# Raw buffers filled ahead of the turned rows' writes, and attention's casts placed behind a norm's squares

## The chip, the cores and the metric

The kernel runs on one core of a Trainium2 chip. The metric is the device time of one execution in microseconds; three runs give a median. A profiled execution gives the trace from which the rows below are taken. In it PE is the matrix engine TensorE, DVE is VectorE, ACT is ScalarE, POOL is GpSimd, and SP is the engine whose queue issues nearly all transfers (its rows are marked SPq). An engine works through its own list of instructions in order, and each instruction waits for what it needs from the others.

## The reference

The program is a two-layer encoder trunk on 256 rows of 1024 float32 numbers. Layer 0 mixes tokens with a convolution module, layer 1 with multi-head latent attention. Each layer is

```
h += 1/2 * SwiGLU(RMSNorm(h))
h += Mixer(RMSNorm(h))
h += 1/2 * SwiGLU(RMSNorm(h))
```

and a last RMSNorm follows. The parts that matter here are the feed-forward and the entry of attention:

```
def swiglu_ffn(h, w1, w3, w2):
    return (jax.nn.silu(h @ w1) * (h @ w3)) @ w2          # 1024 -> 2816 -> 1024

a = h @ w_a                                               # 1024 -> 512 + 256 + 64
c_q  = rmsnorm(a[..., :512], g_q)
c_kv = rmsnorm(a[..., 512:768], g_kv)
k_rope = a[..., 768:]
q  = einsum("bsc,chd->bshd", c_q, w_uq)                   # 8 heads, 128 + 64 rotary
kv = einsum("bsc,chd->bshd", c_kv, w_ukv)                 # 8 heads, 128 keys + 128 values
```

## The kernel before, in words

**Rows and halves.** The 256 rows stand as two tiles `h[0]` and `h[1]` of 128 rows (`tb` 0 and 1). Products are made to full float32 accuracy from three products of rounded parts: a number is split into a high part `hi` and the rest `lo`, and `mm3` (L255) adds hi times lo, hi times hi and lo times hi.

**Weights.** All weights are read once, as a list of blocks of up to 128 x 2048 numbers (1 MB) in the order of use (`blocks`). `load` takes one block: a transfer into one of three raw buffers (`raw`, RAW_BUFS), and then two casts per block half, `hi` on ACT (L173) and `lo` = raw - hi on VectorE (L174), into one of five pairs of weight buffers (W_BUFS). A transfer waits until the raw buffer is free, which is when the `lo` cast of the block three before it has been done; a cast waits until the pair is free, which is when TensorE has finished with the block five before it. `weights(n)` hands out the next n blocks and `load_ahead` loads up to three more.

**Norms.** The RMS factor of a row is not applied to the rows ahead of the product; only the gain is, and the factor comes in behind it. `squares` sums the squares on ACT (L284, two halves), `power` adds the two sums and takes the power -1/2 on POOL (L292, L293, L295), each on one column of 128 numbers. In attention `normed` does the same for the query part (512 columns) and the key part (256) of the first product `a`, with one more POOL step (L1114), and then scales into `cn` on VectorE (L1116).

**Turning rows.** A product needs the rows transposed. For `h[0]` and the attention's parts `split_rows` does it on TensorE (`tp`, L301) and splits into `Xh` (ACT, L315) and `Xl` (VectorE, L319). In layer 1, for `h[1]` at the entries of the first feed-forward, of attention and of the last feed-forward, it goes by transfers: `turn_blocks` makes 32 x 32 transposes on VectorE (`ht`, L330), writes them in four transfers to a DRAM scratch (`hd`, L334) and reads them back in the turned order (`hb`, L336); `Norm.end` then splits `hb` into `Xh` (L397) and `Xl` (L398). This is done in two halves of 512 columns.

**The order around an entry.** `Rows.finish` ends a layer half: four accumulations (tb, d) one after the other, each followed by an addition into `h` (L566, L568) and then by `nxt.early(i)` of the next norm. `Norm.early` turns the first rows by TensorE and begins the turning by transfers (`begin`), the first half at i = 2 and the second at i = 3. Then the next half's first product starts. A feed-forward's `first_chunk` takes the row tiles in the order (w1, tb 0, all eight k), (w3, tb 0, four), (w1, tb 1, eight), (w3, tb 0, four), (w3, tb 1, eight), so that the turned rows are needed after 36 products of `mm3`. Attention takes query tb 0, key tb 0, query tb 1, key tb 1, and then the query's rotary part `qr`, between whose two row tiles stand the transposes of the second query norm and of both key norms (`CQ`, `CKh`, `CKl`). `X.late()` stands where the turned rows are split.

**What sets the order.** The code names the instructions in an order, and a scheduler with its own cost model settles each engine's final list. `urgent` marks functions whose instructions it shall take first; `behind` keeps casts behind the latest urgent work; `order(a, b)` puts a behind b, without any wait of its own where the two are on one engine. Weight transfers that are not needed yet are ordered behind the last `hb` read (`turns`).

Of the kernel before, what the change touches and what calls it, by code (L numbers as in the profile page):

```python
# [19 lines left out]
P = 128  # L20
# [6 lines left out]
HB = 2048  # L27
# [55 lines left out]
def trunk(ctx: ExitStack, tc: tile.TileContext, x, xt, pos, invf, gains, gfin, wdw,  # L83
# [14 lines left out]
    def uid(s):  # L98
        n_uid[0] += 1
        return f"{s}_{n_uid[0]}"  # L100
# [46 lines left out]
    turns = []  # L147
    last_read = [None]

    def load(src, pieces=1):  # L150
        if isinstance(src, tuple):
            raw = rawp.tile([P, HB], F32, tag="raw", name=uid("raw"))
            nc.sync.dma_start(raw, src[1])
            return raw
        n = src.shape[-1]
        raw = rawp.tile([P, HB], F32, tag="raw", name=uid("raw"))
        hi = wp.tile([P, HB], F32R, tag="hi", name=uid("hi"))
        lo = wp.tile([P, HB], F32R, tag="lo", name=uid("lo"))
        if len(loaded) < 7:

            for i in range(pieces if len(loaded) < 4 else 1):
                c = slice(i * n // pieces, (i + 1) * n // pieces) if len(loaded) < 4 else slice(n)
                fetch(raw[:, c], src[:, c])
        else:
            dma = nc.sync.dma_start(raw[:, :n], src)
            if turns and len(loaded) >= n_used[0]:

                order(dma, turns[-1].ins)
        for i in range(pieces):
            c = slice(i * n // pieces, (i + 1) * n // pieces)  # L170

            low = nc.gpsimd if len(loaded) == conv_block[-4] else nc.vector
            casts[len(loaded), i] = (nc.scalar.copy(hi[:, c], raw[:, c]),  # L173
                                     low.tensor_sub(lo[:, c], raw[:, c], hi[:, c].bitcast(F32)))  # L174
            for cast in casts[len(loaded), i]:
                behind(cast)
        return hi, lo
# [128 lines left out]
        return b  # L306

    @urgent
    def split_rows(src, q, n, gcol, dh, dl, tb, after=(), low_after=(), turned=None):

        b = transposed(src, q, n, after, turned)
        for j in range(n):
            k = q + j
            g = G[:, gcol + k:gcol + k + 1]
            high = nc.scalar.activation(dh[:, k, tbs(tb)], b[:, j * P:(j + 1) * P], AF.Copy, scale=g)  # L315
        for j in range(n):
            k = q + j
            g = G[:, gcol + k:gcol + k + 1]
            low = nc.vector.scalar_tensor_tensor(dl[:, k, tbs(tb)], b[:, j * P:(j + 1) * P], g,  # L319
                                                 dh[:, k, tbs(tb)].bitcast(F32), op0=ALU.mult, op1=ALU.subtract)  # L320
            for a in low_after:
                order(low, a.ins)
        return high

    def turn_blocks(pool, src, n, tag):


        w = n * P
        t = pool.tile([P, 512], F32, tag=tag + "t", name=uid(tag + "t"), bufs=2)
        nc.vector.transpose(t[:, :w], src.rearrange("p (t j q) -> p j t q", t=n, q=32))  # L330
        d = dram.tile([P, w], F32, tag=tag + "d", name=uid(tag + "d"), bufs=4)
        dv = d.rearrange("(j p) (i c) -> i p j c", p=32, c=32 * n)
        for i in range(4):
            nc.sync.dma_start(dv[i], t[32 * i:32 * i + 32, :w].rearrange("p (j c) -> p j c", j=4))  # L334
        b = pool.tile([P, 512], F32, tag=tag + "b", name=uid(tag + "b"), bufs=2)
        last_read[0] = nc.sync.dma_start(b[:, :w], d)  # L336
        return b[:, :w].rearrange("p (i t q) -> p t i q", i=4, q=32)

    class Norm:


        def __init__(self, gname, half=False, turn_by_dma=None):
            self.col = GCOL[gname]
            self.half = half

            self.pool = turn_by_dma
            self.turning = []
            self.whole = False
# [4 lines left out]
            self.turned = ()  # L353

            self.between = None

        def part(self, tb, q, after=(), low_after=()):
            turned = self.between if tb == 1 else self.turned if q == 0 and self.turned == [] else None
            self.high = split_rows(h[tb], 4 * q, 4, self.col, self.xh, self.xl, tb, after, low_after, turned)

        @urgent
        def rms(self, tb):
# [176 lines left out]
    class Rows:  # L539
# [20 lines left out]
        def finish(self, rh, make_next, act):  # L560
# [2 lines left out]

            def add(tb, c, o):
                if rh is None:
                    nc.vector.tensor_add(h[tb][:, c], o, h[tb][:, c])  # L566
# [36 lines left out]
    def ffn_in(act, X, make_next, beside):  # L603
# [11 lines left out]
        def first_chunk(X, u):  # L615

            kn = HB // 512
            parts = [weights(2, False) for m in range(2)]
            for m in range(2):
                for tb in range(NT):  # L620
                    u[m, tb] = bank("A", "u")
# [1 line left out]
            for n, (m, tb, ks) in enumerate(((0, 0, range(8)), (1, 0, range(4)), (0, 1, range(8)), (1, 0, range(4, 8)),  # L623
# [3 lines left out]
                elif n == 3:  # L627
                    load_ahead()
                for k in ks:
                    hi, lo = parts[m][k // kn]  # L630
# [448 lines left out]
    def mla_in(act, X, make_next, cc, sn):  # L1079
# [44 lines left out]
                rope(act, kd[:, i, :], kx.rearrange("p (n i f) -> p n i f", n=1, i=2), 1, cc, sn, tb)  # L1124
            return kd.rearrange("p i f -> p (i f)")

        parts = [weights(2, False) for _ in range(2)]
        cq, ck, kd = [], [], []
        last = None
        for tb in range(NT):  # L1130
            for i, w in enumerate((QL, KVL + ROPE)):
                u = low(parts[i], w, tb, last)
# [266 lines left out]
```

## Time and profile before

| | us |
|---|---|
| median of 3 runs | 932.98 |
| lowest and highest run | 931.16, 933.20 |
| the profiled execution, its own time | 932.56 |
| its span, first to last instruction | 930.8 |

The mean granted TensorE clock of the profiled execution is 0.991 of full speed. Times in the rows of a trace are microseconds from the start of the span. A row of the timeline has the start, the length, the engine, the line of the code, the operation, its output and inputs by name, their shape and a count, and in square brackets how long the engine stood idle ahead of it and who ended that. Rows of one kind that follow each other are merged into one, with their count. A row of the waits has the total, the number and the longest. "Granted clock" 0.50 means that TensorE ran at half speed.

### The profile page before, as it was taken

What the parts mean: (1) busy time and instruction counts of PE and PEld (TensorE: products, weight loads), DVE (VectorE), ACT (ScalarE), POOL (GpSimd) and SP (SyncE); (2) the same over time, 40 slices, a digit from 0 to 9 for tenths busy, and PEclk for the clock granted to TensorE, in tenths of its full rate; (3) what the DMA queues carried; (4) which work ended last, traced back from release to release, by engine and by line L of the source; (5) the groups of instructions that cost most, each with busy time, mean ns of one, the idle gap of its engine ahead of it and who ended that gap; (6) DMA issues with size and microseconds to landing.
All of it is one profiled execution on the core that took longest, in us unless ns stands there. A gap on an engine that the chain in (4) does not pass through costs nothing.

```text
span 930.8 us, 12107 instructions
## 1 busy us (share of the span) xinstructions
PE 917.0 (99%) x4346; PEld 768.8 (83%) x4346; DVE 590.2 (63%) x931; ACT 495.5 (53%) x844; POOL 125.5 (13%) x255
## 2 busy tenths in 40 slices
PE   9999999999999999999999999999799999999997
PEld 7888888898978888888888888888698888888886
DVE  5895754489987666654576566545846677656633
ACT  7664443488876444444454554444746575445421
POOL 1720000089941000000010000001300010000000
PEclk9999999999999999999999999999899999999999
DMA  9886775534227677775187776641841288776711
GB/s 342 309 313 223 296 239 207 181 137 165 68 87 271 232 250 247 244 238 208 64 309 288 238 265 240 226 174 39 322 137 46 91 308 308 242 234 233 257 45 46
DMA packets 65292, 194.73 MB, mean 209 GB/s; under 512 B 11856, under 2 KB 37072, under 8 KB 45904
## 3 DMA queue, kind: packets, MB, share of 16 engines
q1 hardware_dynamic: 64656, 193.27, 59.3%
q8 instruction: 34, 0.56, 0.2%
q10 hardware_dynamic: 576, 0.69, 0.2%
q14 instruction: 26, 0.21, 0.1%
HBM read 179.78 MB, written 14.16 MB: 208 GB/s over the span
## 4 chain that ended last, share of the span: by engine, by line
PE 93%; ACT 2%; DMA 1%; DVE 1%; POOL 1%; issue 1%; SPq 0%; POOLq 0%; ACTq 0%; DVEq 0%
PE u L261 17%; PE u L260 17%; PE u L257 17%; PE o L261 9%; PE o L260 9%; PE o L257 9%; PE u L718 3%; PE gate L718 3%; PE o L959 1%; PE u L266 1%; PE tp L301 1%; PE pairs L761 1%; PE nope L257 1%; PE nope L261 1%; PE nope L260 1%; PE sc L1208 1%
## 5 line engine op out<-in xcount | busy, mean ns | idle before, releaser
L174 DVE TENSOR_TENSOR lo<-raw,hi 128x1024 fp32r<-128x1024 f32 (+1 forms) x292 | 344.7, 1219 | 178.0 <-ACT hi L173 177.6
L173 ACT CAST hi<-raw 128x1024 fp32r<-128x1024 f32 x294 | 293.3, 1048 | 250.4 <-PE o L261 82.5
L261 PE MATMUL u<-hi,Xl 128*128 128x512 f32 x688 | 267.8, 389 | 0.3 <-DVE Xl L319 0.3
L257 PE MATMUL u<-lo,Xh 128*128 128x512 f32 x688 | 267.9, 389 | 0.0
L260 PE MATMUL u<-hi,Xh 128*128 128x512 f32 x688 | 267.7, 389 | 0.0
L261 PEld LDWEIGHTS u<-hi,Xl 128*128 128x128 f32 x688 | 129.1, 188 | 27.6 <-DVE Xl L319 0.7
L257 PEld LDWEIGHTS u<-lo,Xh 128*128 128x128 f32 x688 | 129.1, 188 | 26.9
L260 PEld LDWEIGHTS u<-hi,Xh 128*128 128x128 f32 x688 | 129.1, 188 | 26.7
L260 PE MATMUL o<-hi,Gh 128*128 128x512 f32 (+1 forms) x356 | 137.9, 387 | 0.0
L261 PE MATMUL o<-hi,Gl 128*128 128x512 f32 (+1 forms) x356 | 137.8, 387 | 0.0
L257 PE MATMUL o<-lo,Gh 128*128 128x512 f32 (+1 forms) x356 | 137.2, 387 | 0.0
L292 POOL TENSOR_TENSOR ms<-ss 128x1 f32<-128x1 f32 x16 | 10.9, 680 | 602.9 <-ACT junk L284 602.9
L257 PEld LDWEIGHTS o<-lo,Gh 128*128 128x128 f32 x356 | 66.9, 188 | 13.6
L260 PEld LDWEIGHTS o<-hi,Gh 128*128 128x128 f32 x356 | 66.9, 188 | 13.5
L261 PEld LDWEIGHTS o<-hi,Gl 128*128 128x128 f32 x356 | 66.9, 188 | 13.4
L613 DVE TENSOR_TENSOR Gl<-gb,Gh 128x512 fp32r<-128x512 f32 (+1 forms) x48 | 31.3, 652 | 57.3 <-ACT Gh L612 57.3
L612 ACT CAST Gh<-gb 128x512 fp32r<-128x512 f32 (+1 forms) x48 | 28.1, 585 | 73.7 <-DMA gb<-gd 73.7
L795 DVE SCALAR_TENSOR_TENSOR acc<-V,dw,acc 128x128 f32<-128x128 f32 (+1 forms) x176 | 54.6, 396 | 0.0
L816 ACT ACTIVATE prod<-V,dw 128x128 f32<-128x128 f32 (+1 forms) x129 | 46.2, 417 | 1.9 <-POOL Y L817 1.0
L686 DVE TENSOR_TENSOR s<-s,u 128x512 f32<-128x512 f32 (+1 forms) x48 | 30.6, 637 | 7.4 <-PE u L261 7.3
L685 ACT ACTIVATE s<-u,R 128x512 f32<-128x512 f32 (+1 forms) x48 | 31.2, 650 | 5.5 <-PE u L261 4.5
L817 POOL TENSOR_TENSOR odd<-odd,prod 128x128 f32<-128x128 f32 (+1 forms) x62 | 33.0, 536 | 0.0
(213 smaller groups left out, 871.8 us busy)
## 6 DMA issues: line engine op xcount, KB each, us to landing
raw<-in_f2w SPq DMA_DIRECT2D x66, 1024.0 KB, 5.0
raw<-in_f1w SPq DMA_DIRECT2D x62, 1024.0 KB, 5.3
raw<-in_cw SPq DMA_DIRECT2D x12, 1024.0 KB, 4.8
gd<-gt SPq DMA_DIRECT2D x160, 64.0 KB, 3.3
gb<-gd SPq DMA_DIRECT2D x40, 256.0 KB, 4.4
raw<-in_wo SPq DMA_DIRECT2D x4, 1024.0 KB, 4.8
raw<-in_wuq SPq DMA_DIRECT2D x3, 1024.0 KB, 4.8
raw<-in_f1w SPq DMA_DIRECT2D x8, 256.0 KB, 5.5
```

Source lines behind the costliest of these rows:

```text
L173: casts[len(loaded), i] = (nc.scalar.copy(hi[:, c], raw[:, c]), low.tensor_sub(lo[:, c], raw[:, c], hi[:, c].bitcast(F32)))
L174: low.tensor_sub(lo[:, c], raw[:, c], hi[:, c].bitcast(F32)))
L257: mm = nc.tensor.matmul(o, ah, bl, start=start, stop=False)
L260: nc.tensor.matmul(o, ah, bh, start=False, stop=False)
L261: return nc.tensor.matmul(o, al, bh, start=False, stop=stop)
L613: nc.vector.tensor_sub(Gl[:, f, tbs(tb)].rearrange("p t (i q) -> p t i q", q=32), bv, gh.bitcast(F32))
L685: nc.scalar.activation(s[:, :w], u[0, tb][:, :w], AF.Silu, scale=X.r[tb])
L686: nc.vector.tensor_mul(s[:, :w], s[:, :w], u[0, tb][:, w:] if both else u[1, tb])
L718: mm = nc.tensor.matmul(u[:, t], w[:, c], X.x[:, k, t], start=(k == 0), stop=(k == KT - 1))
L795: dve_last.append(nc.vector.scalar_tensor_tensor(out if j == j1 - 1 else y, v, w, y, op0=ALU.mult, op1=ALU.add))
L816: prods_last.append(nc.scalar.activation(p, v, AF.Copy, scale=w))
L817: pool_last.append(nc.gpsimd.tensor_tensor(o, o, p, op=ALU.add))
```

## The change

There are six edits.

1. `raw_to` is new. It issues the transfers of coming blocks into raw buffers without casting them; `load` later finds the buffer in `raws` and only casts.
2. `begin` now does both halves of the turning, and it is called from the next product's code (`first_chunk`, `mla_in`) after three blocks have been handed out. It first issues three transfers by `raw_to`; the `hd` writes of the first half are ordered behind these, and those of the second half behind the first half's `hb` read. `early` no longer begins the turning.
3. Every weight transfer after that is ordered behind the last `hb` read, also those of blocks that are already due.
4. In attention one block is loaded ahead after the first key product (`load_ahead(1)`); the other blocks, which were loaded ahead beside the second query product, now come behind that product's norm.
5. `split_rows` can collect its `Xl` instructions (`lows`), and `Norm.part` does.
6. At the end of attention the last addition into `h` is ordered behind the second of these `Xl`.

```
+    raws = {}
+    def raw_to(last):
+        while len(loaded) + len(raws) < last:
+            src = blocks[len(loaded) + len(raws)]
+            raw = rawp.tile([P, HB], F32, tag="raw", name=uid("raw"))
+            raws[len(loaded) + len(raws)] = raw, nc.sync.dma_start(raw[:, :src.shape[-1]], src)
...
-        raw = rawp.tile([P, HB], F32, tag="raw", name=uid("raw"))
+        there = len(loaded) in raws
+        raw = raws.pop(len(loaded))[0] if there else rawp.tile([P, HB], F32, tag="raw", name=uid("raw"))
...
-            if turns and len(loaded) >= n_used[0]:
+            if turns:
                 order(dma, turns[-1].ins)
...
-    def turn_blocks(pool, src, n, tag):
+    def turn_blocks(pool, src, n, tag, after=()):
...
-            nc.sync.dma_start(dv[i], t[32 * i:32 * i + 32, :w].rearrange("p (j c) -> p j c", j=4))
+            dma = nc.sync.dma_start(dv[i], t[32 * i:32 * i + 32, :w].rearrange("p (j c) -> p j c", j=4))
+            for a in after:
+                order(dma, a.ins)
...
             elif i == 2:
-                if self.pool:
-                    self.begin(0)
                 self.part(0, 1)
                 self.rms(0)
-            elif i == 3 and self.pool:
-                self.begin(1)
-            elif i == 3:
+            elif i == 3 and not self.pool:
                 self.part(1, 0)
 
         @urgent
-        def begin(self, q):
-            self.turning.append(turn_blocks(self.pool, h[1][:, 512 * q:512 * q + 512], 4, "h"))
-            turns.append(last_read[0])
+        def begin(self):
+            raw_to(len(loaded) + RAW_BUFS)
+            first = [dma for raw, dma in raws.values()]
+            for q in range(2):
+                self.turning.append(turn_blocks(self.pool, h[1][:, 512 * q:512 * q + 512], 4, "h", first))
+                first = [last_read[0]]
+                turns.extend(first)
...
             def add(tb, c, o):
                 if rh is None:
-                    nc.vector.tensor_add(h[tb][:, c], o, h[tb][:, c])
+                    ins = nc.vector.tensor_add(h[tb][:, c], o, h[tb][:, c])
+                    if (tb, c.start) == (1, 512):
+                        order(ins, nxt.lows[1].ins)
...
         def first_chunk(X, u):
-            parts = [weights(2, False) for m in range(2)]
+            parts = weights(3, False)
+            X.begin()
+            parts += weights(1, False)
...
-        parts = [weights(2, False) for _ in range(2)]
+        parts = weights(3, False)
+        X.begin()
+        parts += weights(1, False)
...
                 if tb == 0 and i == 1:
                     X.late()
-                elif tb == 1 and i == 0:
-                    load_ahead()
+                    load_ahead(1)
                 if i == 0:
                     cq.append(normed(u, QL, tb))
+                    if tb == 1:
+                        load_ahead()
```

In the settled lists TensorE's and POOL's instructions stand as before. On SP three weight transfers now stand ahead of each entry's first `hd` writes. In attention, ACT has the casts of one block, the squares of the first key norm, `CQ`, the squares of the second query norm, the casts of two blocks, and then the squares of the second key norm; VectorE has the `lo` casts of one block ahead of the first key norm's `cn`, and those of two blocks between the second query norm's `cn` and the second key norm's. In the feed-forwards the casts of three blocks stand ahead of VectorE's first `s`, where there were one and a half.

More of the change, by code (lines that the diff above doesn't have):

```diff
@@ L155, in load @@
         n = src.shape[-1]
-        raw = rawp.tile([P, HB], F32, tag="raw", name=uid("raw"))
+        there = len(loaded) in raws
+        raw = raws.pop(len(loaded))[0] if there else rawp.tile([P, HB], F32, tag="raw", name=uid("raw"))
         hi = wp.tile([P, HB], F32R, tag="hi", name=uid("hi"))
         lo = wp.tile([P, HB], F32R, tag="lo", name=uid("lo"))
-        if len(loaded) < 7:
+        if there:
+            pass
+        elif len(loaded) < 7:
             for i in range(pieces if len(loaded) < 4 else 1):
@@ L308, in split_rows @@
     @urgent
-    def split_rows(src, q, n, gcol, dh, dl, tb, after=(), low_after=(), turned=None):
+    def split_rows(src, q, n, gcol, dh, dl, tb, after=(), low_after=(), turned=None,
+                   lows=None):
         b = transposed(src, q, n, after, turned)
@@ L320, in split_rows @@
                                                  dh[:, k, tbs(tb)].bitcast(F32), op0=ALU.mult, op1=ALU.subtract)
+            if lows is not None:
+                lows.append(low)
             for a in low_after:
@@ L353, in __init__ @@
             self.turned = ()
+            self.lows = []
             self.between = None
@@ L358, in part @@
             turned = self.between if tb == 1 else self.turned if q == 0 and self.turned == [] else None
-            self.high = split_rows(h[tb], 4 * q, 4, self.col, self.xh, self.xl, tb, after, low_after, turned)
+            self.high = split_rows(h[tb], 4 * q, 4, self.col, self.xh, self.xl, tb, after, low_after, turned,
+                                   self.lows)
         @urgent
@@ L629, in first_chunk @@
                 for k in ks:
-                    hi, lo = parts[m][k // kn]
+                    hi, lo = parts[2 * m + k // kn]
                     c = slice(k % kn * 512, k % kn * 512 + 512)
@@ L1131, in mla_in @@
             for i, w in enumerate((QL, KVL + ROPE)):
-                u = low(parts[i], w, tb, last)
+                u = low(parts[2 * i:2 * i + 2], w, tb, last)
                 last = last_low[0]
```

## The prediction

> **What bounds the kernel now.** I read the page's busy times first, then the stretches of the span, then what TensorE waited for.
>
> ```profile
> span 930.8 us, 12107 instructions
> PE 917.0 (99%) x4346; PEld 768.8 (83%) x4346; DVE 590.2 (63%) x931; ACT 495.5 (53%) x844; POOL 125.5 (13%) x255
> ```
> ```profile
> 442.10:465.40 23.30, 23.30 (x108) 19.31 (x107) 12.60 (x21) 10.82 (x23) 1.19 (x4) 1.00 0.19 64
> 465.40:488.70 23.30, 23.30 (x105) 19.28 (x104) 17.11 (x24) 13.92 (x22) 2.97 (x4) 1.00 0.84 309
> 651.60:674.80 23.20, 18.51 (x90) 15.07 (x89) 19.18 (x47) 17.19 (x40) 7.70 (x15) 0.85 0.87 322
> 744.60:767.90 23.30, 23.14 (x102) 19.08 (x103) 16.68 (x29) 16.97 (x30) 3.04 (x8) 1.00 0.83 307
> ```
> ```profile
> PE tp L301 <- DVE cn L1116: 2.8, 2, 2.0
> PE tp L301 <- DVE CKl L319: 1.4, 1, 1.4
> ```
>
> TensorE is the bound nearly everywhere. The columns of a stretch are its bounds, its length, the busy time of PE, PEld, DVE, ACT and POOL, the granted clock, the DMA share and GB/s. The change touches three places where a layer half ends and the next begins: layer 1's first feed-forward (about 463 us), attention (643) and the last feed-forward (744). At the first PE is busy for all of both stretches, so no earlier transfer or cast can gain there. Attention's has 4.69 us of idle PE and a granted clock of 0.85; the last entry has one wait of 0.3 us. These two waits (us in total, times, longest) and two shorter ones shown below, 0.46 for CQ and 0.31 for `Xl`, are all that the change can remove: 5.0 us, and with it the slow clock that follows:
>
> ```profile
> 664.30:667.70 3.40, 1.18 (x8) 0.64 (x6) 2.08 (x3) 2.42 (x4) 2.90 (x8) 1.00 0.87 308
> 667.70:671.10 3.40, 1.54 (x4) 0.82 (x4) 3.36 (x6) 3.33 (x9) 0.00 (x1) 0.50 0.71 229
> 671.10:674.50 3.40, 2.79 (x9) 2.20 (x10) 3.40 (x15) 0.93 (x3) 0.00 (x0) 0.50 0.94 347
> 674.50:677.90 3.40, 3.40 (x13) 3.02 (x13) 3.37 (x8) 0.00 (x0) 0.00 (x0) 0.50 0.43 108
> ```
>
> The clock halves after a stretch with 1.18 of 3.40 us busy, stays halved through one with 2.79 busy, and returns after one that was busy throughout. From 672.2 to 677.9 PE works at half speed, which costs about half of 5.7 us, 2.9 us.
>
> **Where attention loses its 4.7 us.** In order of time, engine by engine:
>
> ```profile
> 657.95 0.39 PE L261 MATMUL a<-hi,Xl 128*128 128x512 f32 x1
> ...
> 666.58 0.88 PE L301 MATMUL tp<-ident,cn 128*128 128x128 f32 x6 [1.97 <-DVE cn L1116]
> 668.27 0.69 PE L301 MATMUL tp<-ident,cn 128*128 128x128 f32 x2 [0.82 <-DVE cn L1116]
> 671.25 0.48 PE L301 MATMUL tp<-ident,kd 128*128 128x128 f32 x1 [1.44 <-DVE CKl L319]
> 672.19 0.79 PE L261 MATMUL qr<-hi,CQ 128*128 128x512 f32 x1 [0.46 <-DVE CQ L319]
> ```
> ```profile
> 658.25 2.01 ACT L173 CAST hi<-raw 128x1024 fp32r<-128x1024 f32 x2
> 660.14 0.50 ACT L284 ACTIVATE junk<-a,R 128x256 f32<-128x256 f32 x1
> 661.22 1.99 ACT L173 CAST hi<-raw 128x1024 fp32r<-128x1024 f32 x2
> ```
> ```profile
> 661.40 3.15 POOL L292 TENSOR_TENSOR ms<-ss 128x1 f32<-128x1 f32 x1 [5.28 <-ACT junk L284]
> 665.54 0.19 POOL L1114 TENSOR_TENSOR rr<-r,R 128x1 f32<-128x1 f32 x1
> ```
> ```profile
> 661.00 3.50 DVE L174 TENSOR_TENSOR lo<-raw,hi 128x1024 fp32r<-128x1024 f32 x3
> 667.74 0.48 DVE L1116 TENSOR_SCALAR cn<-a,rr 128x256 f32<-128x256 f32 x1
> 668.33 2.35 DVE L174 TENSOR_TENSOR lo<-raw,hi 128x1024 fp32r<-128x1024 f32 x2
> 670.59 0.61 DVE L319 SCALAR_TENSOR_TENSOR CKl<-tp,G,CKh 128x128 fp32r<-128x128 f32 x2
> ```
>
> The query norm of the second 128 rows has its squares on ACT behind a cast (from 658.25), then its one-column sum on POOL (L292). That sum takes 3.15 us instead of the usual 0.19: it ends at 664.55, just when VectorE's three casts `lo` end (664.50). While `lo` casts run back to back, POOL does not get through. The key norm follows and its `cn` starts at 667.74; two more casts stand between it and CKl.
>
> **The change, part by part.**
>
> *The squares of the query norm go ahead of the casts.* The changed kernel's instruction order puts only one block's two casts (wuq[2]) ahead of them, and the other two blocks' after. The query product ends at 658.34, so the squares run 658.4 to 659.5 (both halves take 1.1, as 660.14 to the next cast at 661.22 now), POOL's four steps take 1.4 more (the 0.19 steps and one of 0.55), and `cn` can be ready by about 662, when VectorE has done the earlier CQ and rotary pieces. TensorE asks for it at 664.6 (666.58 less the 1.97 of idle). The wait of 1.97 us is gone.
>
> *What is late next.* The two displaced blocks now stand between the query norm and the key norm, on both engines. ACT: 2 x 1.99 us from 659.6 to 663.6, then the key squares, so POOL can begin at about 664.4. (The second of these blocks, wukv[0], is transferred after the last `hb` read, from about 650.5, and 5.3 us later it is there; ACT and the key squares queued behind it would wait only if it came after 661.6.) VectorE: four `lo` casts, from 662.05 at 1.14 us each (3.50 for three with overlap) to 666.6, and only then the key norm's `cn`, in that order. If POOL is held to the end of the last one, as at 661.40, its chain ends 1.2 us later (664.55 to 665.73 now) and `cn` starts at 667.9; if it slips in between casts, at 667.3. Now: 667.74. The bounds are -0.45 and +0.2; I take -0.1, the middle. Behind `cn` nothing is moved: two `lo` casts, CKl, the rotary pieces, CQ, each in the same order. So TensorE does its six transposes 1.3 us earlier, at 665.3, and then waits 2.7 us instead of 0.82. Attention's waits keep their sum, 4.7 us, and so the halved clock behind them stays. Term: -0.1 us.
>
> One row speaks for slipping in between:
>
> ```profile
> 465.58 1.01 POOL L292 TENSOR_TENSOR ms<-ss 128x1 f32<-128x1 f32 x1 [5.97 <-ACT junk L284]
> 465.35 2.32 DVE L174 TENSOR_TENSOR lo<-raw,hi 128x1024 fp32r<-128x1024 f32 x2
> ```
>
> Here POOL ended at 466.59, between two casts. So both happen, which is why I stand in the middle. [...]
>
> *Raw buffers filled ahead (`raw_to`, `begin` after three blocks).* Three transfers of 1 MB now stand in SP's queue ahead of the writes `hd` of the turned rows, and each waits for the `lo` cast that frees its buffer. Where that is close, the writes come late:
>
> ```profile
> raw<-in_f1w SPq DMA_DIRECT2D x62, 1024.0 KB, 5.3
> ```
> ```profile
> 452.22 2.36 DVE L174 TENSOR_TENSOR lo<-raw,hi 128x1024 fp32r<-128x1024 f32 x2 [3.08 <-ACT hi L173]
> ```
> ```profile
> 460.88 1.77 SPq L334 DMA_DIRECT2D hd<-ht  x4
> 465.45 1.75 SPq L334 DMA_DIRECT2D hd<-ht  x4
> 468.59 0.34 SPq L336 DMA_DIRECT2D hb<-hd  x1
> 743.90 3.98 SPq L334 DMA_DIRECT2D hd<-ht  x8
> ```
> ```profile
> DMA to landing us min/median/max: 2.6/2.7/3.2
> ```
>
> At the first entry the third buffer is free at 454.6 and its transfer lands at 459.9, 1.0 us before the writes. At the other two entries the margin is wider (last casts at about 634 and 733, writes at 641.8 and 743.9). The covers hold. If the first cover failed by 1 us, nothing would stop: the turned rows land about 466.8 (460.88, 3.1 from a write to its read as from 465.45 to 468.59, 2.7 to land), and TensorE comes to them 36 products after 463, at 0.22 us (105 in 23.30) near 471. What it buys, casts of the next blocks that no longer wait for a transfer, is worth nothing where PE does not wait. In the two feed-forwards a third block's casts now also stand ahead of the second half's `s` (L685 and L686), which puts it some 2 us later; the PSUM bank that it frees is wanted in the next chunk, 96 products or 21 us after the entry, and `s` runs by 17. Term: 0.
>
> *The last entry: the add ordered behind two of the first `Xl`.*
>
> ```profile
> 742.87 1.14 ACT L315 ACTIVATE Xh<-tp,G 128x128 fp32r<-128x128 f32 x4 [0.35 <-PE tp L301]
> 743.80 0.65 DVE L566 TENSOR_TENSOR h<-o,h 128x512 f32<-128x512 f32 x1
> 744.37 1.11 DVE L319 SCALAR_TENSOR_TENSOR Xl<-tp,G,Xh 128x128 fp32r<-128x128 f32 x4
> 744.76 0.50 PE L261 MATMUL u<-hi,Xl 128*128 128x512 f32 x1 [0.31 <-DVE Xl L319]
> ```
>
> The first `Xl` moves from 744.37 to 743.8, before TensorE wants it at 744.45. The third then comes at about 745.2 and is wanted at 745.8. Gain 0.31 us. Against it: the second `hd` (743.90, eight together) is now ordered behind the first `hb` read. By the same 3.1 us twice and 2.6 to 3.2 for landing, with 0.3 for an issue, the second half lands at 753.0 to 753.6 and, if SP is held 1 us more, at 754.6; its `Xh` follow 0.3 us later, and TensorE wants the first of them 48 products after 743.8, at 754.5. I keep the gain; at the far bound 0.4 us is lost. Term: -0.3, bounds -0.3 and +0.1.
>
> The sum is -0.4 us. The profiled execution took 932.56 us (span 930.8), which gives 932.2; against the median of the runs shown (932.98, 931.16 to 933.2) it gives 932.6. I take **932.4**. About 0.2%, 1.9 us, is what a measurement of this kernel can tell from no change, so the forecast is no measurable change; its own range is 931.2 to 933.2.
>
> **Rivals.**
>
> *Faster: POOL slips through and the clock comes back earlier.* If `cn` of the key norm starts at 667.0 and work resumes at 671.4 instead of 672.19, the stretch 671.1 to 674.5 is almost wholly busy and could lift the clock at 674.5. That saves half of 3.4 us, 1.7, beside 0.4 of wait: 932.4 - 2.1 = 930.3. For it: 2.79 busy of 3.40 was close. Against: VectorE's own four casts end at 666.6. It decides if work resumes by about 671.4. [...] Chance 0.26.
>
> *Slower: the four casts hold the key norm longer than three did.* If the casts on ACT and VectorE start 1 us later than I have them, POOL's chain ends after 668.7, TensorE resumes after 673.1, and the halved clock takes in one more stretch of 3.4 us: 0.5 + 1.7 = 2.2 us, 934.6. For it: everything behind `cn` is in order on VectorE, and POOL was held through three casts. Against: the casts' raws land long before. It decides when the restart slips past a stretch's end. Chance 0.14.
>
> *The change does not do what it says.* No raw transfer runs beside the `hd` writes now, since they are ordered behind the reads; the first part then has nothing to set apart. This is inside the forecast, chance 0.60.
>
> The range reaches to both rivals: 930.0 to 934.4. Faster 0.26, same 0.60, slower 0.14.
>
> **What the profile after would show.** Right: PE's wait for the query `cn` gone, one for the key `cn` of about 2.7 us, the waits for CKl and CQ as before, three halved stretches, and no wait for `Xl` at 744. Wrong: a POOL sum L292 of 0.19 for the key norm with `cn` before 667, fewer halved stretches, a PE wait for `Xh` or `Xl` from `hb`, or raws still landing when `hd` is issued.

## The result, and the profile after

The changed kernel takes 933.97 us in the median of 15 runs (932.35 to 936.51), the kernel before 931.80 in 15 runs (929.99 to 934.31). The ratio is 1.0024 with a 95% interval of 1.0014 to 1.0035: the change makes the kernel slower by 2.2 us. The forecast was no measurable change, a gain of 0.4 us to 932.4. The time lies outside the forecast's own range (931.2 to 933.2) and inside the one stretched towards the rivals (930.0 to 934.4), but the sign was forecast wrongly.

First the busy times of the changed kernel, its stretches (columns as in the prediction) and its waits by TensorE. Its line numbers are higher than those of before: L173 is now L185 (hi), L174 L186 (lo), L284 L296 (squares), L292 L304 (POOL's sum), L1116 L1141 (`cn`), L301 L313 (`tp`), L1072 L1097 (`kd`).

```profile
PE 914.9 (98%) x4346; PEld 767.0 (82%) x4346; DVE 590.1 (63%) x931; ACT 494.8 (53%) x844; POOL 123.4 (13%) x255
```
```profile
465.40:488.70 23.30, 23.30 (x104) 19.28 (x104) 17.48 (x23) 13.64 (x20) 1.86 (x4) 1.00 0.75 256
651.60:674.80 23.20, 15.61 (x76) 12.45 (x75) 17.08 (x43) 16.86 (x40) 6.21 (x13) 0.88 0.53 197
744.60:767.90 23.30, 23.30 (x105) 18.94 (x105) 18.99 (x32) 18.71 (x35) 3.13 (x8) 1.00 0.63 219
```
```profile
PE tp L313 <- DVE cn L1141: 5.7, 2, 5.1
PE tp L313 <- DVE CKl L332: 1.4, 1, 1.4
...
PE qr L273 <- DVE CQ L332: 0.5, 1, 0.5
```

At the other two entries PE is busy throughout, and the 0.31 us for `Xl` at the last entry is gone. Attention's entry is worse: 7.6 us of waits where there were 4.7.

The profiled executions differ by a microsecond or two ahead of attention whatever the edit (a halved clock at 251 us, 3.41 us long in the kernel before, which the last section comes back to, is in some of them and not in others), so I compare by distances from attention's first product (`a`). Each number is the start of an instruction in the trace, less the start of the first `a`:

| kernel | first `a` at | to first `sc` | to first `pv` | to the last FFN's first `u` | to the last `o` |
|---|---|---|---|---|---|
| before | 643.24 | 49.17 | 64.40 | 100.49 | 280.79 |
| after | 642.09 | 52.06 | 67.29 | 103.39 | 283.34 |

From `a` to the last feed-forward the change loses 2.90 us (103.39 - 100.49), and it gains 0.35 behind that (283.34 - 103.39 = 179.95, against 280.79 - 100.49 = 180.30). The sum, +2.55, is near the loss that the medians show (+2.17). The two profiled executions themselves differ by only 1.41 us, because the one of the kernel before has that halved clock at 251 us and the one of the changed kernel has not. The 2.90 is just what TensorE waits longer: 0.56 + 5.13 + 1.44 + 0.46 = 7.59 against 1.97 + 0.82 + 1.44 + 0.46 = 4.69.

```profile
656.80 0.39 PE L273 MATMUL a<-hi,Xl 128*128 128x512 f32 x1
...
664.01 0.88 PE L313 MATMUL tp<-ident,cn 128*128 128x128 f32 x6 [0.56 <-DVE cn L1141]
670.02 0.69 PE L313 MATMUL tp<-ident,cn 128*128 128x128 f32 x2 [5.13 <-DVE cn L1141]
...
673.00 0.48 PE L313 MATMUL tp<-ident,kd 128*128 128x128 f32 x1 [1.44 <-DVE CKl L332]
673.94 0.80 PE L273 MATMUL qr<-hi,CQ 128*128 128x512 f32 x1 [0.46 <-DVE CQ L332]
```
```profile
653.37 1.98 ACT L185 CAST hi<-raw 128x1024 fp32r<-128x1024 f32 x2
...
655.95 1.12 ACT L328 ACTIVATE CQ<-tp,G 128x128 fp32r<-128x128 f32 x4
660.70 0.48 ACT L296 ACTIVATE junk<-a,R 128x256 f32<-128x256 f32 x1 [3.63 <-DVE kd L1097]
...
661.61 3.88 ACT L185 CAST hi<-raw 128x1024 fp32r<-128x1024 f32 x4
665.39 0.37 ACT L296 ACTIVATE junk<-a,R 128x128 f32<-128x128 f32 x1
```
```profile
658.06 0.48 DVE L1141 TENSOR_SCALAR cn<-a,rr 128x256 f32<-128x256 f32 x1 [1.27 <-POOL rr L1139]
...
660.37 0.35 DVE L1097 TENSOR_TENSOR kd<-rp,rp 128x64 f32<-128x64 f32 x2
663.21 0.75 DVE L1141 TENSOR_SCALAR cn<-a,rr 128x512 f32<-128x512 f32 x1 [2.49 <-POOL rr L1139]
663.88 4.62 DVE L186 TENSOR_TENSOR lo<-raw,hi 128x1024 fp32r<-128x1024 f32 x4
669.48 0.48 DVE L1141 TENSOR_SCALAR cn<-a,rr 128x256 f32<-128x256 f32 x1 [0.99 <-POOL rr L1139]
```

The 656.80 row is the last product of the query part on the second 128 rows; it ends at 657.19. ACT has nothing to do from 657.07, and yet it begins the squares only at 660.70: it stands idle for 3.63 us until VectorE's `kd` is done. The squares do not read `kd`. They write their unused result into `junk`, a scratch tile of the ring "s" with two buffers, and the first key part's rotary product `rp` takes both buffers of the same ring (`t1` in `rope`); `kd` is the last to read them. So ACT waits for an old reader of its scratch, and behind ACT wait the two blocks' casts, the key norm's squares, POOL's chain and `cn`.

### The profile page after: what moved, and what is told of

It is laid out like the page before. It is cut to its first block, busy times and chain, and to the rows that moved or that the text cites. A ratio compares the mean times of both kernels' runs of the same rounds, so it can differ in the third digit from the quotient of the medians.

```text
span 932.2 us, 12108 instructions
## 1 busy us (share of the span) xinstructions
PE 914.9 (98%) x4346; PEld 767.0 (82%) x4346; DVE 590.1 (63%) x931; ACT 494.8 (53%) x844; POOL 123.4 (13%) x255
## 4 chain that ended last, share of the span: by engine, by line
PE 91%; DVE 4%; ACT 2%; DMA 1%; POOL 1%; issue 1%; SPq 0%; POOLq 0%; ACTq 0%; DVEq 0%
PE u L272 17%; PE u L273 17%; PE u L269 17%; PE o L269 9%; PE o L272 9%; PE o L273 9%; DVE acc L820 3%; PE u L743 2%; PE gate L743 2%; PE o L984 1%; PE u L278 1%; PE tp L313 1%; PE nope L269 1%; PE nope L273 1%; PE nope L272 1%; PE sc L1236 1%
## 5 line engine op out<-in xcount | busy, mean ns | idle before, releaser
L186 DVE TENSOR_TENSOR lo<-raw,hi 128x1024 fp32r<-128x1024 f32 (+1 forms) x292 | 344.2, 1219 | 176.8 <-ACT hi L185 176.3
L185 ACT CAST hi<-raw 128x1024 fp32r<-128x1024 f32 x294 | 292.5, 1046 | 252.3 <-PE o L273 85.2
L304 POOL TENSOR_TENSOR ms<-ss 128x1 f32<-128x1 f32 x16 | 9.4, 587 | 608.9 <-ACT junk L296 608.9
```

## The experiments

The theories to tell apart. **A**: the shared scratch tile is what costs. **B**: the casts of two blocks between the norms are what costs, whenever the squares begin. **C**: the transfers or the reordered writes cost. All tables of distances and waits below are of one profiled execution each; ratios are to the kernel before, over all runs of the same round.

**A scratch tile of its own**

```
-        t1 = tmp.tile([P, 512], F32, tag="s", name=uid("rp1"))
+        t1 = (tmp.tile([P, 512], F32, tag="s", name=uid("rp1")) if n > 1 else
+              pool.tile([P, 64], F32, tag="rk", name=uid("rp1"), bufs=2))
```

> The changed kernel, with one edit: the key's rotary pieces get a scratch tile of their own instead of the one that they share with the norms' squares. Theory A (the query norm's squares of the second 128 rows wait for that shared tile, which the rotary pieces free only behind a cast block, a norm and CQ): the squares start within 0.3 us of the end of the query product instead of 3.5 us behind it; the key norm's cn starts 9.5 to 10.2 us behind that end instead of 12.3 (before: 9.4); attention's waits of TensorE fall from 7.6 us to about 5; the time is within 0.5 us of before, some 2 us under the change. Theory B (the casts of the two displaced blocks, placed between the query and the key norm, are the delay by themselves): the squares may start earlier, but the key's cn stays at 11.5 us or more, and the time stays 2 us above before.

Measured: 930.81 us (928.87 to 933.33) against 931.92, ratio 0.9985 (0.9972 to 0.9999). ACT and the waits by TensorE:

```profile
659.28 0.48 ACT L296 ACTIVATE junk<-a,R 128x256 f32<-128x256 f32 x1 [0.92 <-PE a L273]
```
```profile
PE tp L313 <- DVE CKl L332: 2.5, 1, 2.5
PE qr L269 <- ACT CQ L328: 1.4, 1, 1.4
...
PE tp L313 <- DVE cn L1142: 0.6, 1, 0.6
```

The squares now follow the query product directly (it ends at 659.15). The key's `cn` comes 9.11 us behind that end, a little earlier than A had it and far from B's 11.5. The waits sum to 4.5 us, and the distance to the last feed-forward falls from 103.39 to 99.81. So A holds: with a scratch tile of its own the loss is gone. Not all of the 3.6 us is the scratch's: 3.05 are waits (7.59 less 4.54), and the scheduler also put two of `qr`'s products ahead of two key transposes, where they run at the full clock (0.50 and 0.40 us, against 0.78 and 0.63 in the changed kernel).

**The changed kernel without the move of the casts**

```
-                    load_ahead(1)
+                elif tb == 1 and i == 0:
+                    load_ahead()
...
-                    if tb == 1:
-                        load_ahead()
```

> The changed kernel, with the edit of attention's casts alone undone: three blocks are loaded ahead beside the second query product, as before; raw buffers are still filled ahead. Theories A and B: the loss of attention goes, the key's cn starts 8 to 9.4 us behind the end of the query product, the time is 0 to 1.5 us under before. Theory C (the transfers filled ahead, with their new place in SP's queue, are what costs): the time stays about 2 us above before.

Measured: 931.64 us, ratio 0.9993 (0.9982 to 1.0005). Attention's waits are 2.7 for `cn`, 1.7 for CKl and 0.2 for CQ, 4.6 against 4.7 before, and the distances are 99.56 to the last feed-forward and 179.95 from there. The key's `cn` comes 9.78 us behind the query product, later than the 8 to 9.4 expected, and without harm. C falls: without the move of the casts, transfers, reordered writes and the last add together cost nothing, and the last add's 0.35 us is here too.

**The move of the casts alone, in the kernel before**

```
-                elif tb == 1 and i == 0:
-                    load_ahead()
+                    load_ahead(1)
...
+                    if tb == 1:
+                        load_ahead()
```

> The kernel before, with the edit of attention's casts alone; transfers and the add stay as before. Theory A: the rotary pieces stand one CQ earlier on VectorE than in the change, so the squares wait less (about 1.5 us behind the product's end instead of 3.5) and the key's cn comes 10 to 10.5 us behind it; the time is about 0.5 to 1 us above before. Theory B: the two blocks' casts stand between the two norms here as well, so the loss is that of the change, 2 to 2.9 us. Theory C: no loss, within 0.3 us of before.

Measured: 932.49 us, ratio 1.0008 (0.9996 to 1.002). The time alone does not decide; the waits do:

```profile
PE tp L301 <- DVE cn L1116: 4.8, 1, 4.8
PE tp L301 <- DVE CKl L319: 1.4, 1, 1.4
...
PE qr L261 <- DVE CQ L319: 0.5, 1, 0.5
PE u L261 <- DVE Xl L319: 0.3, 1, 0.3
```

```profile
655.18 2.00 ACT L173 CAST hi<-raw 128x1024 fp32r<-128x1024 f32 x2 [1.71 <-DMA raw<-in_wuq]
...
659.56 0.47 ACT L284 ACTIVATE junk<-a,R 128x256 f32<-128x256 f32 x1 [1.34 <-DVE kd L1072]
```

The long wait for the key's `cn` comes with this edit alone: 6.7 us in attention, 1.0 us more to the last feed-forward (101.52 against 100.49). ACT's squares wait for `kd` here as well, but 1.34 us instead of 3.63: the first block's `hi` casts (655.18) stand behind the first key norm's squares (652.69), where in the changed kernel they stand in front of them (653.37 and 655.25), so the key's rotary pieces are done earlier against the query product. The key's `cn` comes 11.14 us behind that product, later than A's 10 to 10.5, but the time is A's: 0.6 us above before in the medians, where B had 2 to 2.9. And the 0.3 us for `Xl` are back, since the last add's edit is not in.

So of the 2.90 us lost up to the last feed-forward, 1.03 come with the move of the casts alone, and 1.87 only when the other edits are in as well, although these cost nothing without the move. Here the first block's casts wait for their transfer until 655.18; in the changed kernel that transfer was issued 22 us earlier than in the kernel before (628.48 against 650.47), and its casts went ahead of the squares; why the scheduler set them so is not shown. About half of the 1.87 is waiting (7.59 less 6.66), and most of the rest is where the halved clock fell: here TensorE restarts 6.11 us into it, in the changed kernel 4.50.

**The casts behind the key norm's squares** (with the own scratch tile)

```
                 if i == 0:
                     cq.append(normed(u, QL, tb))
-                    if tb == 1:
-                        load_ahead()
...
+                    if tb == 1:
+                        load_ahead()
```

The added lines stand behind the key's `normed`.

> The changed kernel with a scratch tile of its own for the key's rotary pieces, and with the casts of the two displaced blocks behind the key norm's squares instead of the query norm's. Nothing is left out. Theory B (the casts between the two norms set how late the key's cn comes; measured lags of the key's cn after the query product's end: 9.1 us with two blocks between, 7.6 beside the squares' own delay with one, 5.8 to 6.2 with none): the squares run 0.1 us behind the query product, the key's cn 6.0 to 6.4 us behind it, and TensorE's wait for the key's cn is gone or under 0.5 us. The same 3 blocks of lo casts (2.3 us each on VectorE) then stand between the key's cn and the CKl pieces, so TensorE's wait moves there: 3 to 4.5 us for CKl, and the median stays at 930 to 931.5 us, as with the scratch tile alone (930.8). Rival F (the casts cost only where they hold the norms, since CKl has room): the wait for CKl stays at 1 to 2.5 us, first attention product to first scores is 44 to 46 us against 48.5, and the median is 927.5 to 929 us.

Measured: 933.25 us, ratio 1.0008 (0.9997 to 1.0019).

```profile
662.98 0.48 DVE L1142 TENSOR_SCALAR cn<-a,rr 128x256 f32<-128x256 f32 x1 [1.72 <-POOL rr L1140]
...
668.26 3.49 DVE L186 TENSOR_TENSOR lo<-raw,hi 128x1024 fp32r<-128x1024 f32 x3
671.66 0.60 DVE L332 SCALAR_TENSOR_TENSOR CKl<-tp,G,CKh 128x128 fp32r<-128x128 f32 x2
```
```profile
PE qr L269 <- ACT CQ L328: 3.8, 1, 3.8
PE tp L313 <- DVE CKl L332: 3.1, 1, 3.1
```

As B said, the key's `cn` now comes 5.9 us behind the query product's end (657.08) and TensorE does not wait for it; the casts stand in front of CQ and CKl instead. There they cost more than B had it, and the median is 1.75 us above B's bound (the kernel before took 932.50 in this round, 0.6 more than in the one that B was written from): 6.9 us of waits, 3.1 of them for CKl as expected and 3.8 for CQ on ACT, which B had left out. F falls: the first `sc` comes 50.5 us behind the first `a`, where F had 44 to 46. In both places that were tried between the query product and the last CKl, the casts are in the way.

These traces also give the price of the casts by themselves. From the query product's end to the key's `cn`, with the squares' own delay beside it:

| | blocks cast between the two norms | squares' delay | to the key's `cn` | without the delay |
|---|---|---|---|---|
| before | 1 | 1.80 | 9.40 | 7.60 |
| after | 2 | 3.51 | 12.29 | 8.78 |
| own scratch | 2 | 0.13 | 9.11 | 8.98 |
| move of the casts alone | 2 | 2.22 | 11.14 | 8.92 |
| casts not moved | 0 | 3.98 | 9.78 | 5.80 |
| casts behind the key's squares | 0 | 0.11 | 5.90 | 5.79 |

Two rows compare directly, since their squares start alike: own scratch and casts behind the key's squares. Two blocks cost 9.11 - 5.90 = 3.2 us there. The last column takes the delay off as if it added up one to one, and the three rows with two blocks bear that out (8.78 to 8.98). That the two rows without casts agree as well is partly chance: with the casts not moved a POOL sum took 2.13 us, and in the last row ACT waited 2.47 us for the key product. With that reservation one block costs about 1.8 us, and in the changed kernel 12.29 - 9.40 = 2.89 is 1.71 of delay and 1.18 for the second block. Both have their share, then: the waiting squares are the larger part, as A had it, and the casts' place is a price by itself, though not the whole loss, as B had it.

**The casts set apart.** The own scratch tile; one block fewer loaded between the norms; the second `lo` half of one block, and both casts of the next two, ordered behind the last CKl and CKh:

```
-                        load_ahead()
+                        load_ahead(2)
...
-                split_rows(cq[1], 0, 4, GCOL["q"], CQh, CQl, 1)
+                lows = []
+                split_rows(cq[1], 0, 4, GCOL["q"], CQh, CQl, 1, lows=lows)
...
-                    split_rows(ck[t], 0, 2, GCOL["kv"], CKh, CKl, t)
+                    high = split_rows(ck[t], 0, 2, GCOL["kv"], CKh, CKl, t, lows=lows)
+                b0 = n_used[0] - 1
+                order(casts[b0 + 1, 1][1], lows[-1].ins)
+                for n in (2, 3):
+                    if (b0 + n, 0) in casts:
+                        for i in range(PIECES):
+                            order(casts[b0 + n, i][0], high.ins)
+                            order(casts[b0 + n, i][1], lows[-1].ins)
```

> The changed kernel with own scratch for the key's rotary pieces, and the casts put where neither norm waits for them: wuq[0]'s hi and half its lo behind the query norm, everything else behind the last CKl. By A and B alike the key's cn then starts about 6 us behind the query product's end, TensorE's waits fall from 7.6 to 2 us or less, the clock is not halved, and the time is 4 to 7 us under before. If the clock halves all the same (the eight transposes and the wait around them are enough for that), only 2 to 3 us under before. Theory C: 2 us above before.

Measured: 929.45 us (927.69 to 930.1), ratio 0.9968 (0.9957 to 0.998), faster than both kernels. Attention's entry has 1.0 us of waits and no halved clock; by the first `pv` it is 7.1 us ahead of the kernel before (57.27 against 64.40). The expected gain of 4 to 7 us was missed all the same (2.5 us in the medians): by the last feed-forward only 3.1 are left (97.43 against 100.49). Here is where most of 4 us go, from ACT, PE and the stretches around it:

```profile
718.10 3.88 ACT L185 CAST hi<-raw 128x1024 fp32r<-128x1024 f32 x4
721.88 0.37 ACT L1277 CAST Oh<-pv 128x256 fp32r<-128x256 f32 x1
```
```profile
722.31 0.78 PE L269 MATMUL o<-lo,Oh 128*128 128x512 f32 x1 [1.96 <-ACT Oh L1277]
```
```profile
718.94:722.36 3.42, 1.46 (x11) 0.99 (x9) 3.23 (x4) 3.42 (x6) 0.00 (x0) 1.00 0.45 189
722.36:725.77 3.41, 3.41 (x8) 2.76 (x9) 1.79 (x3) 0.28 (x1) 0.00 (x0) 0.50 0.90 327
```

Two later blocks' casts stand in front of an output copy `Oh` that TensorE needs, and the clock halves behind the gap. The next three kernels ask whether these 4 us can be kept.

**All output copies first.** Both of attention's copies, `ptT` and `Oh`, are put ahead of the casts:

```
+        @urgent
         def probs(pr):
...
+        @urgent
         def values(hd, pt):
```

> The kernel with the casts set apart (own scratch for the key's rotary pieces, one block fewer loaded between the norms, the next blocks' casts behind the last CK pieces), and beside it attention's two kinds of output copies (ptT<-tp and Oh<-pv) put ahead of the casts of the last FFN's blocks in the planner's order. Nothing is left out. Theory D (what that kernel gained by the first pv product, 7.1 us against the kernel before, was given back later because four cast halves of 3.88 us stand ahead of one Oh<-pv on ScalarE: 1.96 us of wait by TensorE at 722 and 3.4 us at half the clock behind it): first pv to the last FFN's first product falls from 40.16 us to the 36.1 us of the kernel before, that wait and that halved stretch are gone, and the median is about 925.5 us (924.5 to 926.5), ratio to the kernel before about 0.993. Rival E (the casts are needed there, and moved back they come late): TensorE waits for hi or lo of the output projection's blocks or of the last FFN's first blocks instead, the stretch stays at 39 to 41 us, and the median is 928.5 to 930.5 us, as without the edit.

Measured: 931.12 us, ratio 0.9984 (0.9974 to 0.9993). D holds for the most part in its own place: first `pv` to the last feed-forward takes 37.41 us instead of 40.15, where D had 36.1. But E's kind of loss comes too, in a place that neither had named, and the median lies above the bounds of both:

```profile
735.93 1.22 DVE L186 TENSOR_TENSOR lo<-raw,hi 128x1024 fp32r<-128x1024 f32 x1
737.06 0.69 DVE L586 TENSOR_TENSOR h<-o,h 128x512 f32<-128x512 f32 x1
737.66 2.35 DVE L186 TENSOR_TENSOR lo<-raw,hi 128x1024 fp32r<-128x1024 f32 x2
...
740.56 0.57 DVE L332 SCALAR_TENSOR_TENSOR Xl<-tp,G,Xh 128x128 fp32r<-128x128 f32 x2
```
```profile
740.92 0.52 PE L273 MATMUL u<-hi,Xl 128*128 128x512 f32 x1 [2.86 <-DVE Xl L332]
```

Pushed back, three halves of `lo` casts stand among the last adds, in front of the norm's first `Xl`; TensorE waits 2.86 us, the clock halves for 3.41 us, and the last feed-forward takes 184.71 us where it took 180.0.

**Two output copies first**, the fourth and the fifth `Oh` only, so that each group of casts is done one copy later and all before the last adds:

```
-                values(i - 3, pt[i - 3])
+                (urgent(values) if i in (6, 7) else values)(i - 3, pt[i - 3])
```

> The kernel with the casts set apart, and beside it only attention's fourth and fifth output copies (Oh<-pv) put ahead of the last FFN's casts in the planner's order, so that the casts are done one copy later each and all lo casts stay ahead of the last adds (where putting every output copy first had pushed two of them in front of the last FFN's Xl: 2.9 us of wait by TensorE there, and the clock halved for 3.4 us behind it). Nothing is left out. Theory D (the 4 us between first pv and the last FFN's first product are a matter of which copy the casts stand in front of): first pv product to the last FFN's first product 36 to 37.5 us, from there to the last product 180.2 to 180.4 us as in all kernels with the edit of the last adds, no halved stretch between 700 and 760, median 925 to 927 us. Rival G (each place for these casts holds some copy that TensorE needs; the loss only moves): a wait of over 1 us by TensorE between 700 and 760 and a halved stretch behind it, median 928.5 to 930.5 us.

Measured: 928.31 us (925.54 to 928.86, 6 runs), ratio 0.9957 (0.9942 to 0.9973).

```profile
PE tp L313 <- DVE CKl L332: 0.7, 1, 0.7
PE o L269 <- ACT Oh L1277: 0.6, 1, 0.6
```
```profile
664.76:668.17 3.41, 2.21 (x11) 1.11 (x10) 3.29 (x16) 3.12 (x10) 0.08 (x1) 1.00 0.00 0
668.17:671.58 3.41, 3.41 (x12) 2.92 (x12) 3.41 (x8) 3.21 (x5) 0.00 (x0) 0.50 0.03 7
700.00:760.00 60.00, 59.44 (x302) 49.08 (x301) 40.20 (x87) 37.91 (x87) 3.03 (x8) 1.00 0.45 162
```

The part asked about came out by D: 37.23 us from `pv` to the last feed-forward, 179.95 behind it, and from 700 to 760 the clock is full and PE idle for 0.56 us. The median, 928.3, is above the 925 to 927 of D, and by the interval no different from the casts set apart alone. The profile shows one cause in its own execution: with about the same waits at attention's entry as the kernel with the casts set apart (1.1 us, of which 0.7 for CKl, and 1.0), it got a halved stretch at 668.17 that the other did not, and its first `pv` is 1.8 us later (59.08 against 57.27). Whether that holds in the other executions isn't shown.

**One output copy first**, the fourth alone (`if i == 6` in the same line):

> As the kernel with two output copies put first, but with the fourth alone, so that four halves of hi casts (3.88 us) stand in front of the fifth copy, as they do in the kernel before at 724.82, where TensorE does not wait for it. Nothing is left out. Theory D: no wait by TensorE over 0.5 us there, first pv product to the last FFN's first product 36 to 37.5 us, median 925 to 927 us. Rival G: TensorE waits 1 to 2 us for that copy and the clock halves for 3.4 us behind it: 39 to 40.5 us, median 928.5 to 930.5 us.

Measured: 926.75 us in the median of five executions (926.48 to 929.17), ratio 0.9956 (0.9941 to 0.9971), by the intervals no different from two. The sixth, which was the profiled one, took 5298 us, so no row can say what TensorE waits for there, and the wait that D and G differ on stays open.

## Why the prediction was wrong, point by point

**The squares of the query norm: the step that failed.** "So the squares run 658.4 to 659.5" took the query product and ACT's own list as the only things that they wait for. The order on ACT was right; what was missed is the buffer: the squares need a scratch tile back from VectorE's rotary pieces. Measured, they begin 3.51 us behind the product, not at once. The kernel before has the same shared tile, but its squares begin 1.80 us after the product behind a cast (the row at 660.14 has no idle time), and the first `kd` was over at 659.93:

```profile
659.70 0.23 DVE L1072 TENSOR_TENSOR kd<-rp,rp 128x64 f32<-128x64 f32 x1
```

The cover of the wait was the very cast that the change takes away. The wait for the query's `cn` fell from 1.97 to 0.56 where the forecast had it gone, and what stands behind the squares came later than forecast with them.

**What is late next.** The mechanism was right: two blocks' casts stand on ACT and VectorE between the norms, and TensorE's long wait is for the key's `cn`. The forecast put `cn` at 667.9 for a product end of 658.34, 9.6 us behind it; with the scratch tile set apart, 9.11 was measured, and 12.29 with it shared. So the term -0.1 (bounds -0.45 and +0.2) came out as +2.9, outside its bounds, and the part beyond them is the squares' lateness. Where the step above is made true, attention's waits are 4.54 us, against the forecast 4.7, and the kernel is 0.15% faster than before. That the sums are so near is partly luck: the forecast had 2.7 for `cn`, 1.44 for CKl and 0.46 for CQ, and measured were 0.57, 2.54 and 1.43. One reading of the prediction contradicts its own rows: the six transposes were to come 1.3 us earlier, at 665.3, but without the wait of 1.97 they come at 664.6. The 2.7 fits the latter, and no term hangs on it.

**POOL.** I took the middle between a sum held to the end of the casts and one that slips in. In the changed kernel it slips in once:

```profile
666.28 1.14 POOL L304 TENSOR_TENSOR ms<-ss 128x1 f32<-128x1 f32 x1 [3.10 <-ACT junk L296]
667.50 1.05 POOL L305 TENSOR_SCALAR ms<-ms 128x1 f32<-128x1 f32 x1
668.63 0.55 POOL L307 TENSOR_TENSOR r<-ms,neghalf 128x1 f32<-128x1 f32 x1
```

VectorE's four `lo` run from 663.88 to 668.50. The first step, usually 0.19 us, ends about with the third cast and the second with the fourth, and each takes about as long as one cast (1.14 and 1.05 us, against 4.62 / 4 = 1.16); the chain ends 0.95 us behind the last cast, where the forecast had 1.2 for a sum held to the end. In the kernel before, a sum took 3.15 us, and with the casts not moved 2.13, both longer than one cast. Why POOL takes longer there is not shown.

**The clock.** Three halved stretches, 10.24 us, were forecast and came, from 669.44; TensorE restarts 4.50 us into them (673.94), as in the kernel before (672.19 - 667.70 = 4.49). Against the kernel before, the whole loss is waiting, none of it the clock.

**Raw buffers ahead, and `s` later: right by themselves.** No wait for a transfer or an `Xh` from `hb` appears, PE is full at the first entry, and the kernel with these edits and the old place of the casts is at 0.9993 of before. The term of 0 holds as long as the casts stay; with the casts moved, the earlier transfer has a part in the 1.87 us above, which the prediction, taking its parts one by one, could not see. The rival by which this part has nothing to set apart is borne out as far as that: at attention's entry no weight transfer was issued between the writes and the reads of the turned rows before the change either.

**The last add: right.** -0.30 was forecast, and -0.35 measured in the changed kernel and in all others with the edit but two: -0.31 with the casts set apart, and with all output copies first it is hidden by the wait for `Xl`. The far bound, a late `hb`, did not come in.

**The rivals.** The slower one had the mechanism, casts that begin later and hold the key norm, and a loss of 2.2 us; that the size came out is luck, since the parts are others: the casts begin 4.42 us behind the query product (661.61) where the forecast had 1.26 and the rival 2.26, and no further stretch is halved. Its chance, 0.14, was too small because "the casts' raws land long before" was taken as the only thing that could make them late. The faster one, an earlier end of the halved clock, did not come in the changed kernel; two halved stretches instead of three appear in the kernels with the scratch set apart and with the casts not moved (6.83 us each). The range was said to reach to both rivals, but it ends at 934.4 and the slower one stands at 934.6.

## What to carry to other kernels

Before an instruction is moved ahead, list everything it waits for, the reuse of its output and scratch buffers included: an output that nobody reads still needs a free buffer (the squares waited 3.63 us for theirs), and the cover of that wait may be the work that is being moved. And where an engine in the way has slack only on average, moving its work finds the next consumer: two blocks' casts made the key's `cn` 3.2 us later, left 6.9 us of waits in front of CQ and CKl, and later casts 2.0 in front of `Oh` and 2.9 in front of `Xl`, until each group stood in a gap. The order that held for the whole chain (scratch apart, casts behind the last CKl, two copies first) is 0.43% faster than the kernel before.

## What the runs showed of the hardware that was not expected

In some of these traces a halved clock followed on short waits, so that they cost TensorE more than their length. In the kernel with the casts set apart, 1.96 us of waiting in a stretch of 3.42 us was followed by 3.41 us at half the clock; in the one with two copies first, a stretch with 2.21 us busy was too, though its single waits were at most 0.68 us. The other, with 1.01 us of waits at the same place, was not halved there. The halved stretches ahead of the program's end in these traces last 3.41, 6.83 or 10.24 us: one, two or three steps of 3.41. The busy time of the stretch ahead did not decide it alone: with a scratch tile of its own, a stretch with 1.98 us busy was not followed by a halved one.

At one place the halved clock went with where the work fell against these steps. Some 390 us ahead of attention TensorE runs 16 products `ms` that are one column wide; they take 2.4 us from about 249. In five of the nine traces, that of the kernel before among them, these products lie within one stretch but for at most 0.3 us (an estimate, with bounds worked out from the later halved stretches in steps of 3.41 us; in the kernel before, the two halved stretches begin at 251.27 and 667.70, and the 416.43 us between them are 122 steps of 10.24 / 3), and the clock is halved behind it, for 3.41 us or once 6.83, although PE counts as busy for 3.22 of 3.41 us before it in the kernel before (247.86 to 251.27). In the four others, that of the changed kernel among them, they reach by the same estimate at least 0.5 us into each of two stretches, and the clock stays full. From the first `ms` to attention's first `a` it is 394.3 to 394.8 us in the five and 393.2 to 393.3 in the four. So with the same 16 products the way to attention took 1.0 to 1.6 us longer in the five traces with the halved clock than in the four without it.
